# The return of expert outputs moved into the next pair's gate projection, its buffers shared, one more weight unit

## The chip, the cores and the metric

The kernel runs on one core of one Trainium2 chip. The metric is the device time of one execution in microseconds; the time before is the median of three runs. The engines are TensorE (PE in the profile, its weight loads PEld), VectorE (DVE), ScalarE (ACT), GpSimd (POOL) and SyncE (SP), which issues the weight transfers.

## The reference

A two-layer decoder trunk on 256 tokens of width 1024, in float32. Layer 1 of the reference (layer 0 in the code) is multi-scale retention with 4 heads, layer 2 (layer 1 in the code) is block attention with 8 heads over 256 tokens. Each is followed by a mixture of experts, which is what the change touches:

```python
g_val, g_idx = lax.top_k(g_prob, 1)
e_val, e_idx = lax.top_k(e_logits, EXPERT_TOPK)      # 2 of the 4 experts of one of 4 groups
hg = silu(einsum('td,edf->tef', t, w_gate[g])) * einsum('td,edf->tef', t, w_up[g])
y = y + einsum('tef,efd->td', hg * combine[:, g, :, None], w_down[g])
```

There are 16 experts of hidden width 512, and every token goes to two of them. A final RMS norm ends the trunk. The weights are about 250 MB, and the kernel reads them all.

## The kernel before, in words

**Order.** Retention, experts of layer 0, attention, experts of layer 1. The dense stages split each weight into two float32r parts (L337 to L341) and multiply three times (L345 to L347).

**Weights.** All weights pass through a ring of 1 MB units (class Ring, L158 and L147 are its issues). A unit is a [128, 2048] float32 tile, 8 KB in each partition. In an expert stage the ring has 19 slots of its own, further ones that other tiles leave (flex_slot, slot_v, h) and N_EXTRA more. SP issues the units in order; an issue waits until the last reader of its slot is done, and until the transfer eight issues earlier has landed.

**Expert pairs.** moe(layer) works through 8 pairs of experts. A pair has 12 units: gate, up and down, 4 each. Each expert takes up to 64 tokens, so the two experts of a pair fill the 128 rows of a tile, expert s in rows 64 s to 64 s + 63. The two sides are multiplied as 64-column matmuls (tile 128x64) side by side: expand (L982) for gate and up into a PSUM bank each (tag ps, 2 banks), project (L1010) for down into two banks (tag pt, 2 banks). Each float32 matmul is two instructions in the trace.

**Steps of one pair j** (loop at L1227), in TensorE's order, which is written out by hand here as is ScalarE's (manual_schedule); VectorE's, GpSimd's and SP's order is the framework's:

1. silu of the gate by ScalarE in two halves (L1204), then up (L982, 8 k steps), then gate() multiplies in two halves on VectorE (L1210).
2. turn_in: the tokens of pair j + 1, which were fetched into xn, are transposed by 4 + 4 transposes (L953) into two pt banks and written to xg, one half by VectorE (L940), the other by ScalarE in four pieces (L944).
3. turned: the hidden tile is transposed by 4 transposes into one ps bank (L997) and copied to hd, columns 0 to 255 by VectorE (L999) and 256 to 511 by ScalarE (L1000).
4. scatter: the return of pair j - 1, 8 matmuls of full width (L1029, L1030) which add its outputs to the four accumulators total, through the 0/1 matrix ST.
5. slots(j + 2): two small matmuls (L960) give the token numbers of pair j + 2, and pull (L947) lets GpSimd fetch these tokens from DRAM by an indirect DMA into xn.
6. project (L1010): the down projection.
7. parts: the outputs are split into yh by ScalarE (L1021) and yl by VectorE (L1022), four tiles of 2 KB each.
8. Gate of pair j + 1 (L982). In the last but one pair a branch for experts with more than 64 tokens (more, L1106) stands in the middle of it.

The return of the last pair follows its own down projection (L1259, or L1038 to L1071 in finish with the final norm).

**Waits.** The framework makes a wait for each dependence that it sees between instructions of different engines. For a tile of PSUM the rows below show which instructions of other engines a reader waited for.

**Buffers.** flex 2 and 3 hold the two float32r parts of the dense stages' input (8 KB each); in the expert stages flex 3 holds xn and xg together (held), and flex 0 to 2 are ring slots. Tiles of tag work (2 buffers of 2 KB) take the hidden tile and its transpose in turn.

Of the kernel before, what the change touches and what calls it, by code (L numbers as in the profile page):

```python
# [10 lines left out]
F32 = mybir.dt.float32  # L11
# [184 lines left out]
def trunk(ctx, tc, x, x_t, dense_in, moe_in, gain_in, par_in, fin_in, rot_in, dec_in, con_in, out):  # L196
    nc = tc.nc
    V = nc.vector
    N_BASE, N_FLEX, N_EXTRA = 20, 2, 0
# [13 lines left out]

    def x_parts():
        return flex(2, [128, KD, T], F32R, "xh"), flex(3, [128, KD, T], F32R, "xl")
# [51 lines left out]
    ident_b = const.tile([128, 128], BF16, name="ident_b")  # L267
# [192 lines left out]
    def retention():  # L460
        with tc.tile_pool(name="ret_w", bufs=2, reuse_waits="tile") as wpool:
# [98 lines left out]
            for n, (a, b, unit, pieces) in enumerate(FIRST):  # L560
# [3 lines left out]
                if n == 0:  # L564
# [14 lines left out]
            nc.gpsimd.affine_select(out=ident_b, in_=ones_b, compare_op=OP.is_equal, fill=0.0, base=0,  # L579
                                    pattern=[[-1, 128]], channel_multiplier=1)  # L580
# [187 lines left out]
    def router(layer, junk):  # L768
# [34 lines left out]
    def moe(layer):  # L803
        g0 = G_FFN[layer]
        with tc.tile_pool(name="extra", bufs=1, side="right", reuse_waits="tile") as late, \
# [172 lines left out]
            def expand(sides, xg, p, name, ks, weight, done):  # L978
                w = 128 // len(sides)
                for k in ks:  # L980
                    for s in sides:
                        nc.tensor.matmul(p[s * w:(s + 1) * w], xg[:, k, s * w:(s + 1) * w], weight(name, k, s),  # L982
                                         start=(k == 0), stop=(k == KD - 1))
                    done(name, k)
# [18 lines left out]
            def project(sides, hd, weight, done):  # L1003
                w = 128 // len(sides)
                yp = [pt(), pt()]
                for ks in ((0, 1), (2, 3)) if len(sides) > 1 else ((0,), (1,), (2,), (3,)):
                    for n in range(2):
                        for k in ks:
                            for s in sides:
                                nc.tensor.matmul(yp[n][s * w:(s + 1) * w], hd[:, k, s * w:(s + 1) * w],  # L1010
                                                 weight("d", k, s)[:, n * 512:(n + 1) * 512],
                                                 start=(k == 0), stop=(k == 3))
                    for k in ks:
# [65 lines left out]
            def slots(j, bank=pt):  # L1079
                RS[j], idx = slot_values(sel_of(j), [cs[:, tt, j] for tt in range(NT)],  # L1080
                                         [con[:, C_SELC + 12 * n:C_SELC + 12 * n + 12] for n in range(2)], bank)
                if j:
                    pull(idx, xn)
# [14 lines left out]
            def grow(j, name, ks):  # L1098
# [244 lines left out]
```

## Time and profile before

| | us |
|---|---|
| median of 3 runs | 742.85 (742.61 to 743.23) |
| the profiled execution | 742.91 |
| its span, first to last instruction | 740.9 |
| TensorE busy | 720.5 (97%) |
| VectorE busy | 320.1 (43%) |
| ScalarE busy | 270.4 (36%) |
| GpSimd busy | 35.9 (5%) |
| granted TensorE clock, mean | 0.997 of full |

The span is cut in 40 slices of 18.5 us in the page's second part; a digit is the busy share of a slice in tenths. The expert stages run from about 209 to 412 us (layer 0) and from about 527 us to the end (layer 1). In the timeline a line is one instruction or several alike behind each other: start, length until the last has ended, engine, line of the kernel, what is written from what, the shape, the count, and in brackets the idle time before and what ended it. Matmuls overlap, so the start of the next line, not the length, tells how long a group held TensorE.

### The profile page before, as it was taken

The page shows a single profiled execution, that of the slowest core. Times are in us where ns is not written, and L with a number is a line of the kernel's source. Part 1 is how long each engine was busy: PE and PEld are TensorE (multiplying, and loading weights), DVE is VectorE, ACT ScalarE, POOL GpSimd, SP SyncE. Part 2 cuts the span into 40 slices and gives each one's busy share as a digit, 9 for nine tenths or more (in the row PEclk, how much of TensorE's full clock was granted, in tenths as well). Part 3 has the DMA queues.
Part 4 walks back from the last instruction along what each step waited for, and adds up shares of the span by engine and source line. Part 5 has one row for each costly group of instructions (what it writes and reads, how often), then busy time and mean ns, then how long its engine had stood idle before and what let it go on. Part 6 is the DMA issues. An engine that isn't in the chain of part 4 may idle for free.

```text
span 740.9 us, 10093 instructions
## 1 busy us (share of the span) xinstructions
PE 720.5 (97%) x3652; PEld 430.1 (58%) x3652; DVE 320.1 (43%) x893; ACT 270.4 (36%) x550; POOL 35.9 (5%) x48
## 2 busy tenths in 40 slices
PE   8999999999999999999999999999999999999984
PEld 6988898887863434443343688888733344434431
DVE  4976688667661202211110677765721121112103
ACT  5667554667431111111110778674411111111112
POOL 0000000001000000000000003130010000000000
PEclk9999999999999999999999999999999999999998
DMA  8999646577879999999999799757899999999993
GB/s 246 421 420 420 228 145 243 207 278 274 323 283 388 422 419 419 419 423 419 419 421 404 315 422 421 290 211 303 318 397 421 420 421 418 423 419 421 420 410 122
DMA packets 43366, 263.24 MB, mean 355 GB/s; under 512 B 5695, under 2 KB 6975, under 8 KB 13616
## 3 DMA queue, kind: packets, MB, share of 16 engines
q1 hardware_dynamic: 40752, 256.85, 86.5%
q0 software_dynamic: 2560, 5.71, 2.1%
q8 instruction: 30, 0.49, 0.3%
q14 instruction: 24, 0.20, 0.1%
HBM read 263.12 MB, written 3.15 MB: 359 GB/s over the span
## 4 chain that ended last, share of the span: by engine, by line
PE 62%; DMA 34%; DVE 2%; issue 1%; SPq 0%; ACT 0%; DVEq 0%; POOLq 0%; ACTq 0%
DMA slot<-in_moe_dram 22%; PE ps L982 10%; PE acc L347 10%; PE acc L345 10%; PE acc L346 10%; DMA h<-in_moe_dram 8%; PE pt L1010 7%; DMA held<-rows,idx 2%; PE acc L383 2%; PE acc L381 2%; PE acc L382 2%; PE ps L794 1%; DMA slot<-in_dense_dram 1%; PE pt L953 1%; PE pt L884 1%; PE acc L1030 1%
## 5 line engine op out<-in xcount | busy, mean ns | idle before, releaser
L982 PE MATMUL ps<-slot,held 128*64 128x512 f32 x816 | 184.8, 594 | 2.0 <-DMA slot<-in_moe_dram 1.6
L982 PEld LDWEIGHTS ps<-slot,held 128*64 128x64 f32 x816 | 58.5, 137 | 116.7 <-issue 104.7
L341 DVE SCALAR_TENSOR_TENSOR wlo<-slot,gain,whi 128x512 fp32r<-128x512 f32 x144 | 107.0, 752 | 37.4 <-ACT whi L340 35.8
L340 ACT ACTIVATE whi<-slot,gain 128x512 fp32r<-128x512 f32 x144 | 102.9, 721 | 55.4 <-PE acc L346 37.0
L1210 DVE SCALAR_TENSOR_TENSOR gl<-ps,rs,gl 128x256 f32<-128x256 f32 x32 | 14.0, 480 | 194.5 <-PE ps L982 194.5
L1010 PE MATMUL pt<-slot,hd 128*64 128x512 f32 x416 | 96.2, 596 | 1.0 <-DVE idx L962 0.5
L345 PE MATMUL acc<-whi,xh 128*128 128x512 f32 x224 | 91.1, 407 | 0.6 <-ACT whi L340 0.6
L346 PE MATMUL acc<-whi,xl 128*128 128x512 f32 x224 | 87.6, 391 | 0.0
L347 PE MATMUL acc<-wlo,xh 128*128 128x512 f32 x224 | 87.5, 393 | 0.1
L1022 DVE TENSOR_TENSOR yl<-pt,yh 128x512 fp32r<-128x512 f32 x32 | 22.1, 691 | 99.9 <-ACT yh L1021 99.9
L1021 ACT ACTIVATE yh<-pt 128x512 fp32r<-128x512 f32 x32 | 19.1, 597 | 115.5 <-PE pt L1010 115.5
L1010 PEld LDWEIGHTS pt<-slot,hd 128*64 128x64 f32 x416 | 28.5, 137 | 53.1 <-issue 51.1
L944 ACT ACTIVATE held<-pt,gain 128x128 f32<-128x128 f32 x60 | 17.2, 368 | 102.5 <-PE pt L953 99.0
L1204 ACT ACTIVATE gl<-ps,rs 128x256 f32<-128x256 f32 x32 | 13.4, 470 | 106.3 <-PE ps L982 106.3
L347 PEld LDWEIGHTS acc<-wlo,xh 128*128 128x128 f32 x224 | 42.0, 188 | 10.0 <-DVE wlo L341 0.5
L345 PEld LDWEIGHTS acc<-whi,xh 128*128 128x128 f32 x224 | 42.2, 188 | 8.9 <-ACT whi L340 0.9
L346 PEld LDWEIGHTS acc<-whi,xl 128*128 128x128 f32 x224 | 42.2, 188 | 8.2
L338 DVE TENSOR_TENSOR wlo<-slot,whi 128x512 fp32r<-128x512 f32 x44 | 30.2, 689 | 21.0 <-ACT whi L337 18.2
L337 ACT ACTIVATE whi<-slot 128x512 fp32r<-128x512 f32 x44 | 27.8, 632 | 28.3 <-DVE wlo L338 16.3
L381 PE MATMUL acc<-xh,whi 128*128 128x256 f32 x128 | 35.9, 281 | 1.7 <-ACT whi L340 1.7
L383 PE MATMUL acc<-xh,wlo 128*128 128x256 f32 x128 | 36.2, 284 | 0.4 <-DVE wlo L341 0.3
L382 PE MATMUL acc<-xl,whi 128*128 128x256 f32 x128 | 35.6, 279 | 0.0
(226 smaller groups left out, 933.1 us busy)
## 6 DMA issues: line engine op xcount, KB each, us to landing
slot<-in_moe_dram SPq DMA_DIRECT2D x152, 1024.0 KB, 19.8
slot<-in_dense_dram SPq DMA_DIRECT2D x43, 1024.0 KB, 17.5
flex_slot<-in_moe_dram SPq DMA_DIRECT2D x22, 1024.0 KB, 19.8
slot_v<-in_moe_dram SPq DMA_DIRECT2D x8, 1024.0 KB, 19.6
h<-in_moe_dram SPq DMA_DIRECT2D x6, 1024.0 KB, 19.8
slot<-in_dense_dram SPq DMA_DIRECT2D x16, 256.0 KB, 6.4
rows<-h POOLq DMA_DIRECT2D x2, 1024.0 KB, 8.8
flex_slot<-in_moe_dram SPq DMA_DIRECT2D x4, 512.0 KB, 17.7
```

The costliest lines, as they stand in the source:

```text
L337: nc.scalar.activation(hi, w, AF.Copy)
L338: V.tensor_tensor(lo, w, hi.bitcast(F32), op=OP.subtract)
L340: nc.scalar.activation(hi, w, AF.Copy, scale=g)
L341: V.scalar_tensor_tensor(lo, w, g, hi.bitcast(F32), op0=OP.mult, op1=OP.subtract)
L345: nc.tensor.matmul(p, a, wh, start=start, stop=False)
L346: nc.tensor.matmul(p, l, wh, start=False, stop=False)
L347: nc.tensor.matmul(p, a, wl, start=False, stop=stop)
L381: nc.tensor.matmul(d, wh[:, s], xh[:, k], start=(k == 0 and c % 2 == 0), stop=False)
L382: nc.tensor.matmul(d, wh[:, s], xl[:, k], start=False, stop=False)
L383: nc.tensor.matmul(d, wl[:, s], xh[:, k], start=False, stop=(k == KD - 1 and c % 2 == 1))
L982: nc.tensor.matmul(p[s * w:(s + 1) * w], xg[:, k, s * w:(s + 1) * w], weight(name, k, s), start=(k == 0), stop=(k == KD - 1))
L1010: nc.tensor.matmul(yp[n][s * w:(s + 1) * w], hd[:, k, s * w:(s + 1) * w], weight("d", k, s)[:, n * 512:(n + 1) * 512], start=(k == 0), sto ...
```

## The change

- The return of pair j stands after the first two k steps of the gate of pair j + 1, and no longer before the down projection of pair j + 1.
- The fetch of pair j + 2 is issued after that return and no longer right after its slots.
- Up's last two k steps are done for columns 0 to 255 and then for columns 256 to 511.
- turn_in and turned alternate: four input transposes, two of the hidden tile, four, two. ScalarE copies the first half of the hidden tile, VectorE the second. In the last pair the second two hidden transposes stand inside the down projection (between).
- flex 3 is cut in two tiles of 4 KB, flex 3 (xg) and flex 4. Flex 4 holds in turn the fetched tokens (xn) and the first half of the split outputs (ylow); the second half uses the work tiles. The four ys tiles, one of two ST tiles and the constant ident_b go. Halves makes the two tiles look like one in the dense stages.
- N_EXTRA is 1: one more ring slot of 8 KB in the expert stages.

```diff
-    N_BASE, N_FLEX, N_EXTRA = 20, 2, 0
+    N_BASE, N_FLEX, N_EXTRA = 20, 2, 1
...
+    def rows_in():
+        return flex(4, [128, D], F32, "xn")
...
-        held = flex(3, [128, 2, D], F32, "held")
-        xn = held[:, 0]
-        xg = held[:, 1].rearrange("p (k j) -> p k j", k=KD)
+        xg = flex(3, [128, D], F32, "xg").rearrange("p (k j) -> p k j", k=KD)
+        xn = rows_in()
...
-            def turned(hh, hd, bank=ps):
+            def turned(hh, hd, t, n):
                 hv = hh.rearrange("t (k p) -> t k p", k=4)
-                t = bank()
-                for k in range(4):
-                    nc.tensor.transpose(t[:, k * 128:(k + 1) * 128], hv[:, k], ident)
                 tv = t.rearrange("p (k j) -> p k j", k=4)
-                V.tensor_copy(hd[:, 0:2], tv[:, 0:2])
-                nc.scalar.activation(hd[:, 2:4], tv[:, 2:4], AF.Copy)
-                return hd
+                for k in (2 * n, 2 * n + 1):
+                    nc.tensor.transpose(tv[:, k], hv[:, k], ident)
+                s = slice(2 * n, 2 * n + 2)
+                if n:
+                    V.tensor_copy(hd[:, s], tv[:, s])
+                else:
+                    nc.scalar.activation(hd[:, s], tv[:, s], AF.Copy)
...
+                low = flex(4, [128, 2, 512], F32R, "ylow")
                 for n in range(2):
-                    ys.append([t1(name, [128, 512], F32R, bufs=4, tag="ys") for name in ("yh", "yl")])
+                    ys.append([work(name, F32R) if n else low[:, i] for i, name in enumerate(("yh", "yl"))])
...
-                    grow(j, "u", range(0, 8))
+                    grow(j, "u", range(0, 6))
+                    for s in halves:
+                        grow(j, "u", range(6, 8), s)
                     gate(hh, GU[j, "u"], rs)
+                    hd, t, idx, between = work("hd").rearrange("p (k j) -> p k j", k=4), ps(), None, None
                     if j + 1 < NP:
                         for n in range(2):
                             turn_in(xn, xg, range(4 * n, 4 * n + 4), COLS[n])
-                    hd = turned(hh, work("hd").rearrange("p (k j) -> p k j", k=4))
-                    if ahead:
-                        scatter(*ahead)
-                    if j + 2 < NP:
-                        slots(j + 2, ps)
-                    yp = project(both, hd, weight_of(j), done_of(j))
-                    st = transposed_select(rs, t1("ST", [128, T], F32R, bufs=2))
-                    if j + 2 < NP:
-                        ahead = parts(yp), st
-                        grow(j + 1, "g", range(0, 8))
-                    elif j + 1 < NP:
-                        ahead = parts(yp), st
-                        grow(j + 1, "g", range(0, 4))
+                            turned(hh, hd, t, n)
+                        if j + 2 < NP:
+                            idx = slots(j + 2, ps)
+                    else:
+                        turned(hh, hd, t, 0)
+
+                        def between():
+                            turned(hh, hd, t, 1)
+
+                    st = transposed_select(rs, t1("ST", [128, T], F32R))
+                    yp = project(both, hd, weight_of(j), done_of(j), between)
+                    if j + 1 < NP:
+                        ys = parts(yp)
+                        grow(j + 1, "g", range(0, 2))
+                        scatter(ys, st)
+                        if j + 2 < NP:
+                            xn = rows_in()
+                            pull(idx, xn)
+                            grow(j + 1, "g", range(2, 8))
+                            continue
+                        grow(j + 1, "g", range(2, 4))
```

project calls between() once, after the first half of its first output bank.

## Rows read from the trace of the kernel before

**Rows 1.** The page: TensorE's busy line, the transfers' share in 40 slices, the chain that ended last by engine.
```profile
PE 720.5 (97%) x3652; PEld 430.1 (58%) x3652; DVE 320.1 (43%) x893; ACT 270.4 (36%) x550; POOL 35.9 (5%) x48
...
DMA  8999646577879999999999799757899999999993
...
PE 62%; DMA 34%; DVE 2%; issue 1%; SPq 0%; ACT 0%; DVEq 0%; POOLq 0%; ACTq 0%
```
**Rows 2.** TensorE's timeline over one pair in the middle of layer 1: the end of up, input transposes (L953), hidden transposes (L997), the first two and (by the next line's start) all matmuls of the return, slots (L960), down projection (L1010), gate of the next pair.
```profile
566.55 5.32 PE L982 MATMUL ps<-slot,held 128*64 128x512 f32 x24
571.80 1.09 PE L953 MATMUL pt<-ident,held 128*128 128x128 f32 x8
572.73 0.64 PE L997 MATMUL ps<-ident,gl 128*128 128x128 f32 x4
573.12 0.48 PE L1029 MATMUL acc<-yh,ST 128*128 128x512 f32 x1
573.44 0.39 PE L1030 MATMUL acc<-yl,ST 128*128 128x512 f32 x1
...
575.05 0.21 PE L960 MATMUL ps<-cs,S 128*128 128x13 bf16 x2
575.19 1.08 PE L1010 MATMUL pt<-slot,hd 128*64 128x512 f32 x4
...
582.11 5.32 PE L982 MATMUL ps<-slot,held 128*64 128x512 f32 x24
```
**Rows 3.** The chain of waits in order of time: the gate and up matmuls of the next pair as one piece (start, length, what).
```profile
582.28 13.73 PE ps L982 x64
```
**Rows 4.** TensorE's timeline at the end of layer 0 and of layer 1: the start of the last pair's gate, the branch, the last up matmuls, the last turn (layer 1), the end of the moved return (layer 1), the start of the last down projection; then, in layer 1, the end of that projection and the return behind it.
```profile
385.01 1.89 PE L982 MATMUL ps<-slot,held 128*64 128x512 f32 x8
...
388.77 5.37 PE L982 MATMUL ps<-slot,held 128*64 128x512 f32 x24 [0.16 <-PEq L1106]
...
398.41 1.94 PE L982 MATMUL ps<-slot,held 128*64 128x512 f32 x8 [0.54 <-DMA slot<-in_moe_dram]
...
403.59 3.65 PE L1010 MATMUL pt<-slot,hd 128*64 128x512 f32 x16
...
702.81 1.89 PE L982 MATMUL ps<-flex_slot,held 128*64 128x512 f32 x8
...
716.87 1.94 PE L982 MATMUL ps<-slot,held 128*64 128x512 f32 x8 [0.54 <-DMA slot<-in_moe_dram]
...
719.54 0.74 PE L997 MATMUL ps<-ident,gl 128*128 128x128 f32 x4 [0.73 <-DVE gl L1210]
...
721.74 0.40 PE L1030 MATMUL acc<-yl,ST 128*128 128x512 f32 x1
722.07 1.08 PE L1010 MATMUL pt<-slot,hd 128*64 128x512 f32 x4
...
728.13 1.03 PE L1010 MATMUL pt<-slot,hd 128*64 128x512 f32 x4
729.09 0.50 PE L1029 MATMUL acc<-yh,ST 128*128 128x512 f32 x1
729.42 0.39 PE L1030 MATMUL acc<-yl,ST 128*128 128x512 f32 x1
```
**Rows 5.** Busy time in one stretch of 4 us at the start of the experts of layer 0: us, PE, PEld, DVE, ACT, POOL busy (instructions), granted clock, DMA share, GB/s.
```profile
212.00:216.00 4.00, 4.00 (x36) 3.29 (x36) 3.55 (x21) 1.02 (x4) 0.00 (x0) 1.00 0.50 199
```
**Rows 6.** The page's groups of instructions: the split of the down projection's output, on VectorE and on ScalarE (busy us, mean ns of one, idle before).
```profile
L1022 DVE TENSOR_TENSOR yl<-pt,yh 128x512 fp32r<-128x512 f32 x32 | 22.1, 691 | 99.9 <-ACT yh L1021 99.9
L1021 ACT ACTIVATE yh<-pt 128x512 fp32r<-128x512 f32 x32 | 19.1, 597 | 115.5 <-PE pt L1010 115.5
```
**Rows 7.** VectorE and ScalarE in the timeline of the same pair as rows 2: the gate's two halves, the first input copy, the two halves of the hidden tile's copy.
```profile
572.00 0.88 DVE L1210 SCALAR_TENSOR_TENSOR gl<-ps,rs,gl 128x256 f32<-128x256 f32 x2 [12.49 <-PE ps L982]
...
572.79 0.68 DVE L940 TENSOR_TENSOR held<-pt,gain 128x512 f32<-128x512 f32 x1
...
573.40 0.42 DVE L999 COPY hd<-ps 128x256 f32<-128x256 f32 x1
...
574.01 0.40 ACT L1000 ACTIVATE hd<-ps 128x256 f32<-128x256 f32 x1
```
**Rows 8.** The view of waits (who waited for whom: us in total, times, longest) for readers of a PSUM bank that another instruction uses at other columns. L708 reads columns 0 to 127 and L709 columns 128 to 255 of an attention score tile, whose columns 128 to 383 L705 writes.
```profile
ACT hd L1000 <- DVE hd L999: 17.3, 2, 9.1
...
ACT slot L709 <- DVE slot L708: 3.1, 3, 1.0
...
DVE slot L708 <- PE ps L705: 1.6, 3, 0.7
...
DVE held L940 <- ACT held L944: 0.4, 2, 0.2
```
**Rows 9.** Float32 matmuls of 256 columns in the attention stage: two of them and the start of what follows on TensorE.
```profile
483.33 0.59 PE L736 MATMUL ps<-slot,slot 128*128 128x256 f32 x2
...
483.76 0.38 PE L737 MATMUL ps<-slot,slot 128*128 128x128 f32 x2
```
**Rows 10.** The token fetches (L947), all 14: us from the start of the fetch on GpSimd to its landing.
```profile
DMA to landing us min/median/max: 8.1/8.6/9.1
```
**Rows 11.** TensorE's timeline in the first pair of layer 0: input transposes after the fetch, and the down projection.
```profile
231.22 1.06 PE L953 MATMUL pt<-ident,held 128*128 128x128 f32 x8 [0.65 <-DMA held<-rows,idx]
...
233.23 7.09 PE L1010 MATMUL pt<-slot,hd 128*64 128x512 f32 x32 [0.48 <-DVE idx L962]
```

More of the change, by code (lines that the diff above doesn't have):

```diff
@@ L212, in flex_slot, with __init__, __getitem__ @@
         return flex(n, [128, 2048], F32, f"flex_slot{n}")
+    class Halves:
+        def __init__(self, parts):
+            self.parts = parts
+        def __getitem__(self, at):
+            p, ks, *rest = at
+            if isinstance(ks, int):
+                return self.parts[ks // 4][(p, ks % 4, *rest)]
+            n = ks.start // 4
+            assert ks.stop <= 4 * n + 4
+            return self.parts[n][(p, slice(ks.start - 4 * n, ks.stop - 4 * n), *rest)]
     def x_parts():
-        return flex(2, [128, KD, T], F32R, "xh"), flex(3, [128, KD, T], F32R, "xl")
+        return flex(2, [128, KD, T], F32R, "xh"), Halves([flex(3 + n, [128, 4, T], F32R, f"xl{n}") for n in range(2)])
+    def rows_in():
+        return flex(4, [128, D], F32, "xn")
     def acc():
@@ L976, in transposed_select, with expand @@
                 return st
-            def expand(sides, xg, p, name, ks, weight, done):
+            def expand(sides, xg, p, name, ks, weight, done, at=slice(0, FE)):
                 w = 128 // len(sides)
@@ L981, in expand @@
                     for s in sides:
-                        nc.tensor.matmul(p[s * w:(s + 1) * w], xg[:, k, s * w:(s + 1) * w], weight(name, k, s),
-                                         start=(k == 0), stop=(k == KD - 1))
-                    done(name, k)
+                        nc.tensor.matmul(p[s * w:(s + 1) * w, at], xg[:, k, s * w:(s + 1) * w],
+                                         weight(name, k, s)[:, at], start=(k == 0), stop=(k == KD - 1 and at.stop == FE))
+                    if at.stop == FE:
+                        done(name, k)
             def glu(gp, up, rs, hh):
@@ L991, in glu, with project @@
                 return hh
-            def turned(hh, hd, bank=ps):
+            def turned(hh, hd, t, n):
                 hv = hh.rearrange("t (k p) -> t k p", k=4)
-                t = bank()
-                for k in range(4):
-                    nc.tensor.transpose(t[:, k * 128:(k + 1) * 128], hv[:, k], ident)
                 tv = t.rearrange("p (k j) -> p k j", k=4)
-                V.tensor_copy(hd[:, 0:2], tv[:, 0:2])
-                nc.scalar.activation(hd[:, 2:4], tv[:, 2:4], AF.Copy)
-                return hd
-            def project(sides, hd, weight, done):
+                for k in (2 * n, 2 * n + 1):
[5 more added lines that the diff above has]
+                    nc.scalar.activation(hd[:, s], tv[:, s], AF.Copy)
+            def project(sides, hd, weight, done, between=None):
                 w = 128 // len(sides)
@@ L1012, in project @@
                                                  start=(k == 0), stop=(k == 3))
+                        if between:
+                            between()
+                            between = None
                     for k in ks:
@@ L1081, in slots @@
                                          [con[:, C_SELC + 12 * n:C_SELC + 12 * n + 12] for n in range(2)], bank)
-                if j:
-                    pull(idx, xn)
+                return idx
             def weight_of(j):
@@ L1096, in done_of, with grow @@
                 return done
-            def grow(j, name, ks):
+            def grow(j, name, ks, at=slice(0, FE)):
                 if (j, name) not in GU:
                     GU[j, name] = ps()
-                expand(both, xg, GU[j, name], name, ks, weight_of(j), done_of(j))
+                expand(both, xg, GU[j, name], name, ks, weight_of(j), done_of(j), at)
             def more():
@@ L1190, in more @@
                         half = [e2_[:, n * FE:(n + 1) * FE] for n in range(4)]
-                        lhd = turned(glu(*lp2, lrs, half[0]), e0[:, D:D + 512].rearrange("p (k j) -> p k j", k=4), pt)
+                        lhd = e0[:, D:D + 512].rearrange("p (k j) -> p k j", k=4)
+                        lhh, lt = glu(*lp2, lrs, half[0]), pt()
+                        for n in range(2):
+                            turned(lhh, lhd, lt, n)
                         y = half[2:]
@@ L1207, in gate @@
             def gate(hh, up, rs):
-                for c in range(2):
-                    s = slice(c * 256, (c + 1) * 256)
+                for s in halves:
                     V.scalar_tensor_tensor(hh[:, s], up[:, s], rs[:, 1:2], hh[:, s], op0=OP.mult, op1=OP.mult)
+            halves = [slice(c * 256, (c + 1) * 256) for c in range(2)]
             with tc.manual_schedule(engines={mybir.EngineType.PE}):
@@ L1233, in moe @@
                         nc.scalar.activation(small.tile([128, 1], F32, name="root1"), ident[:, 0:1], AF.Sqrt)
-                    grow(j, "u", range(0, 8))
+                    grow(j, "u", range(0, 6))
+                    for s in halves:
+                        grow(j, "u", range(6, 8), s)
                     gate(hh, GU[j, "u"], rs)
+                    hd, t, idx, between = work("hd").rearrange("p (k j) -> p k j", k=4), ps(), None, None
                     if j + 1 < NP:
```

6 lines of the change are left out of this document (1 added, 5 removed).

## The prediction

> **What bounds the kernel now.** I read the page first. TensorE is busy 97% of the span and the transfers are nearly full in both expert layers, so either could be the limit, and the chain of waits gives 34% to DMA [rows 1]. The reader is to see next that this share misleads. TensorE's timeline of one expert pair in the middle of layer 1 has no hole: up matmuls from 566.55, transposes at 571.80, the return (scatter) at 573.12, the down projection at 575.19, the next gate projection at 582.11 [rows 2]. The chain has 64 gate and up matmuls in 13.73 us, 0.2145 each [rows 3]. So up ends at E = 566.55 + 24 x 0.2145 = 571.70, the down projection starts at P = 575.19, 3.49 after E, of which the return takes 573.12 to 575.05 = 1.93 and the rest 1.56.
>
> Does TensorE wait for weights at all? Only in the last pair of each layer [rows 4]. Layer 0's last gate starts at 385.01; 64 matmuls and the 0.33 hole of the branch (388.77 against 385.01 + 16 x 0.2145 = 388.44) would end up at 399.07; it ends at 398.41 + 8 x 0.2145 = 400.13. Layer 1: 702.81 gives 716.87, and it is 718.59. So the transfers hold TensorE 1.06 and 1.72 us, 2.8 in all; everything else in the expert stages is TensorE's own order.
>
> **The extra weight unit.** Transfers do stand idle for a moment at the start of each expert stage (share 0.50 in layer 0, [rows 5]); a unit more in flight there can bring later units forward. It can shorten only those 2.8 us. I value it at nothing, since the moved return alone puts the last up matmuls behind the last landings (below); its bounds are 0 and 2.8.
>
> **The return inside the gate projection.** Eight matmuls at (575.05 - 573.44)/7 = 0.23 stay eight matmuls. What changes is the neighbours. Today it stands behind transposes of the same 128-column shape and pays 0.09. Now it stands between 64-column matmuls. The end of layer 1 shows both edges [rows 4]: down projection to return, last group 728.13 + 4 x 0.2145 = 728.99, return at 729.09, second matmul 0.33 later where 0.23 is usual, so 0.20; return to down projection, 721.74 + 0.23 = 721.97 against 722.07, and about 0.05 lost in the first group, so 0.15. In its new place the return costs 8 x 0.23 + 0.35 = 2.19, 0.26 more, seven times a layer. Bounds 0 and 0.5. Its operands are no wait: the last one is ready 0.28 + 0.60 + 0.69 = 1.6 us after the down projection (ScalarE's split, then VectorE's, [rows 6]; 0.28 is worked out below) and is used at 1.72 + 0.2 + 0.9 = 2.8.
>
> **The turns.** Now: four input transposes, two of the hidden tile, four, two, the next slots, the down projection. Three waits decide. (a) Hidden transposes need the first gated half. Up's last quarter is split so that this half could be gated early, but both halves lie in one PSUM bank. The rows say that the program waits by bank: a VectorE read of columns 0 to 127 waited for the matmul on columns 128 to 383 (L708 for L705), a ScalarE read of other columns waited for that VectorE read (L709 for L708), and so did the two halves of the hidden tile's copy (L1000 for L999) and of the input's (L940 for L944) [rows 8]. So the gate starts as now, at 572.00, 0.30 after E [rows 7], and the first hidden transpose at 0.95 after E, as in the last pair (718.59 to 719.54, [rows 4]); today eight input transposes hide that, in the new order four (until 0.63) do not. (b) The first two hidden transposes end at 1.15 (0.10 each, (573.12 - 572.73)/4, [rows 2]); ScalarE starts 0.28 later, as VectorE does at 573.40, and copies for 0.40 [rows 7]: 1.83. The other two write the same bank, so by the same rule they wait for that copy: 1.88 to 2.08. No row shows a TensorE write held by a reader of other columns; without this wait they follow the input transposes at 1.55. (c) Slots 0.14, down projection at E + 2.22. That is 0.66 more than 1.56 (bounds 0, and 0.8). The input's first copy, 572.79 plus 0.68, is done by then.
>
> The PSUM rule matters here. The Trainium skill, page "PSUM — Partial Sum Buffer", section "PSUM bank collisions raise a hardware error", says that two engines may not touch one bank in the same quadrant of partitions at once, whatever the columns, and that accesses are to be guarded by bank. By it the wait in (b) is needed too and the sum is the one below; by columns alone it would be that of the third rival.
>
> **Edits at nothing.** The half-width matmuls: 256 columns in f32 run at (483.76 - 483.33)/2 = 0.215 each, their weight loads hidden [rows 9], so sixteen at half width replace eight at the same time. The upper bound is a bare load in each of eight steps, at most the 0.14 of a two-matmul slots step, 1.1 us a pair. The Trainium skill, page "TensorE: Matmul & The Clock Gate", section "The mechanism", says that weight loads overlap running matmuls only in another row group; both sides here share theirs. By it the loads would be bare; the 0.2145 of [rows 3] speaks against it. The fetch of the next tokens is now queued on POOL behind the return's first half: 1.72 + 0.2 + 0.9 + 0.3 = 3.1 after the down projection; with at most 9.1 to landing [rows 10] it is there at 12.2, and is wanted after gate, return and up at 13.73 + 2.19 + 0.1 = 16.0. That cover is 3.8. Nothing else of weight is queued on POOL. SP's issues keep their order, the extra one among them. Splitting the buffers and dropping one constant touch no chain.
>
> **First and last pair.** The first pair has no gate wait (up ended while the tokens were fetched) but a hole of about half a microsecond before its down projection. By (b): 231.22 + 0.53 + 0.20 + 0.28 + 0.40 + 0.05 + 0.20 + 0.14 = 233.02 against 233.23 [rows 11]: 0.2 gained. In the last pair the down projection starts at 0.95 + 0.20 + 0.28 + 0.40 + 0.05 = 1.88 after E, and the two later transposes stand inside it at 0.35 (two shape changes as above, two at 0.10).
>
> **Sum.** End of the last up matmuls without weight waits, then the changes: -0.2, six turns at 0.66 = 3.96, seven returns at 2.19 less six at 1.93 = 3.75; together +7.51. Layer 0: 399.07 + 7.51 + 1.88 + 0.35 = 408.81 against the down projection's start at 403.59 [rows 4]: +5.2. Layer 1: 716.87 + 9.74 = 726.61 against 722.07: +4.5. The last up matmuls would begin near 404.9 and 722.7, well behind their weights' landings at 398.41 and 716.87, and the down units behind them are wanted later than now, so no weight wait is left. Layer 0's loss passes on whole, since the attention stage starts from its result. 742.91 + 9.7 = 752.7 for an execution like the profiled one, which is 0.06 above the median: 752.6.
>
> **Rivals.**
> - *Only the gate waits by bank* (TensorE isn't held by ScalarE's copy). For: no row shows that wait. Against: every pair of engines in [rows 8] does wait. The down projection starts at E + 1.89, 0.33 less in twelve pairs and 0.2 in two: 748.2.
> - *Loads become bare in the half-width matmuls.* 1.1 x 16 = 18 more: about 770. Against it: [rows 3, 9].
> - *Columns are told apart.* The gate's first half runs beside up's second, turned and input transposes hide each other's copies, as the order is meant: twelve turns 0.61 less, two last pairs 0.85 less, the first pairs 0.3 less: 743.0, no change.
> - *The other side: the return fills the time in which TensorE waited for weights.* As the last rival, and the edges of the return inside the gate cost nothing: 14 x 0.26 less, 739.4, faster. It decides from the point where a moved return plus its edges cost less than the 2.8 us of waits. For: those waits and the bare 0.95 after the last up are in the rows. Against: the edges in [rows 4] and the waits in [rows 8].
> - *The change doesn't do what it says* (no room for the unit, or a late fetch) is inside these, as the unit is worth nothing in the first.
>
> **Chances and range.** Forecast 0.64, gate alone 0.10, bare loads 0.04, columns told apart 0.11, faster 0.11. About 0.2%, 1.5 us, is what a measurement of this kernel tells from no change. Faster takes the fifth and a sliver of the fourth, 0.12; the rest of the fourth and a little beside it is no change, 0.12; slower 0.76. The forecast's own range, with 0.1 either way on twelve turns and on fourteen returns, is 749.8 to 755.4. The range that leaves out no more than the faster case, the bare loads and a rest is 742.8 to 756.
>
> **What would show it.** In the changed profile: down projection about 2.2 after the last up matmul of a middle pair, with the second pair of hidden transposes waiting for ScalarE's copy and the first for the gate; the gate starting after both halves; returns of about 2.2 from gate to gate; no weight waits in the last pairs; the fetch landed before it is wanted. I am wrong if the gate starts while up still runs, if a middle pair takes 24.2 us or less, or if TensorE still waits for weights at the end.

## The result and the profile after

The changed kernel takes 752.76 us (median of 4 runs, 752.58 to 753.29) where the kernel before took 742.73 in the same comparison: ratio 1.0137, 95% interval 1.012 to 1.0155. It is slower by 10.0 us. The profiled execution has 752.77 us, a span of 750.7 (740.9 before) and a granted clock of 0.996 (0.997).

The page of the changed kernel, the lines that answer to [rows 1]:

```profile
PE 729.5 (97%) x3780; PEld 439.7 (59%) x3780; DVE 321.5 (43%) x893; ACT 272.0 (36%) x550; POOL 35.4 (5%) x47
...
DMA  7999546478799999999998997567999999999981
...
PE 3%; DVE 1%; ACT 0%; DVEq 0%; issue 0%
```

TensorE is still busy 97%, of a span that grew with it, so this share can't show where 10 us went. Nor can the chain of waits: its shares add up to 4% of the span, where the kernel before has 99% [rows 1]. It was followed back only to 719.16, the last pair's gate behind the branch, and says nothing of the time ahead of that. That DMA is missing in it is therefore no finding; what became of the waits for weights is read from TensorE's timeline below.

The timeline of one pair in the middle of layer 1, with TensorE, VectorE, ScalarE and GpSimd; it answers to [rows 2, 7]. L964 is an input transpose, L1009 a hidden one, L971 the slots, L1023 the down projection, L993 gate and up, L1046 and L1047 the return, L1228 the gate's multiplication, L1014 ScalarE's copy:

```profile
578.48 0.66 PE L964 MATMUL pt<-ident,xn 128*128 128x128 f32 x4
578.67 0.88 DVE L1228 SCALAR_TENSOR_TENSOR gl<-ps,rs,gl 128x256 f32<-128x256 f32 x2 [11.71 <-PE ps L993]
579.30 0.41 PE L1009 MATMUL ps<-ident,gl 128*128 128x128 f32 x2 [0.17 <-DVE gl L1228]
...
579.55 0.60 PE L964 MATMUL pt<-ident,xn 128*128 128x128 f32 x4
579.75 0.38 ACT L1014 ACTIVATE hd<-ps 128x256 f32<-128x256 f32 x1 [7.20 <-PE ps L1009]
...
580.19 0.44 PE L1009 MATMUL ps<-ident,gl 128*128 128x128 f32 x2
580.46 0.20 PE L971 MATMUL ps<-cs,S 128*128 128x13 bf16 x2
580.59 1.08 PE L1023 MATMUL pt<-slot,hd 128*64 128x512 f32 x4
...
587.51 1.89 PE L993 MATMUL ps<-slot,xg 128*64 128x512 f32 x8
589.32 0.50 PE L1046 MATMUL acc<-ylow,ST 128*128 128x512 f32 x1
...
591.03 0.99 POOL L958 DMA_INDIRECT xn<-rows,idx  x1 [24.09 <-PE acc L1047]
...
591.37 5.37 PE L993 MATMUL ps<-slot,xg 128*64 128x512 f32 x24
...
603.55 0.66 PE L964 MATMUL pt<-ident,xn 128*128 128x128 f32 x4
```

Read it from one input transpose to the next: 603.55 - 578.48 = 25.07 a pair. The kernel before has 595.94 - 571.80 = 24.14, from this row of its next pair and the one in [rows 2]:

```profile
595.94 1.09 PE L953 MATMUL pt<-ident,held 128*128 128x128 f32 x8
```

From the first input transposes to the down projection it is 2.11; before it was 575.19 - 571.80 = 3.39, of which the return took 1.93, so 1.46 [rows 2]. The gate starts 0.19 after the input transposes, as before, although up is split. The second pair of hidden transposes starts at 580.19, just behind ScalarE's copy (579.75 + 0.38 = 580.13). The return costs from 587.51 + 8 x 0.2145 = 589.23 to 591.37, 2.14.

The end of layer 1 on TensorE's timeline, answering to [rows 4]:

```profile
717.06 1.94 PE L993 MATMUL ps<-slot,xg 128*64 128x512 f32 x8
719.16 1.94 PE L993 MATMUL ps<-slot,xg 128*64 128x512 f32 x8 [0.16 <-PEq L1122]
...
727.77 1.93 PE L993 MATMUL ps<-slot,xg 128*64 128x256 f32 x16
730.43 0.41 PE L1009 MATMUL ps<-ident,gl 128*128 128x128 f32 x2 [0.74 <-DVE gl L1228]
731.31 1.94 PE L1023 MATMUL pt<-slot,hd 128*64 128x512 f32 x8 [0.47 <-ACT hd L1014]
733.18 0.44 PE L1009 MATMUL ps<-ident,gl 128*128 128x128 f32 x2
733.55 5.37 PE L1023 MATMUL pt<-slot,hd 128*64 128x512 f32 x24
738.85 0.50 PE L1046 MATMUL acc<-ylow,ST 128*128 128x512 f32 x1
```

No up matmul waits for a transfer any more. In the last pair nothing hides the waits of the turn: 0.74 for the gate and 0.47 for the copy.

Most experiments move single microseconds, and executions of one kernel differ by as much outside the expert stages. So each is also read by its own profiled stages: from the first gate matmul of a layer to its last down projection, from there to layer 1's first gate matmul, and to the end of the span. The last column is the turn of a middle pair of layer 1, from the first input transposes to the down projection, without the return. All are differences of starts in TensorE's timelines; the column to the end is good to 0.1 only, as the spans are given to 0.1.

| kernel | layer 0 | layer 1 | between | to the end | turn |
|---|---|---|---|---|---|
| before | 188.65 | 189.36 | 129.12 | 18.8 | 1.46 |
| changed | 193.13 | 193.47 | 129.65 | 19.4 | 2.11 |
| return alone | 193.87 | 193.78 | 129.12 | 18.9 | 2.08 |
| turns alone | 190.15 | 190.21 | 129.94 | 19.4 | 2.05 |
| up whole | 193.05 | 193.41 | 129.92 | 19.3 | 2.11 |
| two banks | 191.34 | 191.34 | 129.64 | 19.3 | 1.86 |
| four banks | 188.51 | 188.88 | 129.65 | 19.4 | 1.57 |
| no extra slot (1st, 2nd) | 193.11, 193.11 | 193.47, 193.47 | 129.66, 129.66 | 20.1, 20.1 | |
| last return (1st, 2nd) | 187.81, 187.82 | 187.78, 188.52 | 129.41, 129.43 | 18.8, 18.8 | |
| last return, first and last pair split | 187.33 | 187.25 | 129.42 | 19.1 | |
| last return, last pair split | 186.94 | 186.96 | 129.45 | 18.9 | |

The changed kernel's excess is 4.48 + 4.11 + 0.53 + about 0.5 and 0.12 ahead of the first gate: about 9.8, the difference of the spans.

### The profile page after: what moved, and what is told of

It is laid out like the page before. It is cut to its first block, busy times and chain, and to the rows that moved or that the text cites. A ratio compares the mean times of both kernels' runs of the same rounds, so it can differ in the third digit from the quotient of the medians.

```text
span 750.7 us, 10355 instructions
## 1 busy us (share of the span) xinstructions
PE 729.5 (97%) x3780; PEld 439.7 (59%) x3780; DVE 321.5 (43%) x893; ACT 272.0 (36%) x550; POOL 35.4 (5%) x47
## 5 line engine op out<-in xcount | busy, mean ns | idle before, releaser
L993 PE MATMUL ps<-slot,xg 128*64 128x512 f32 (+1 forms) x904 | 181.2, 542 | 0.3 <-PEq L1122 0.3
L993 PEld LDWEIGHTS ps<-slot,xg 128*64 128x64 f32 x904 | 65.2, 137 | 105.5 <-issue 91.9
L1023 PE MATMUL pt<-slot,hd 128*64 128x512 f32 x416 | 93.6, 596 | 0.5 <-ACT hd L1014 0.5
L1228 DVE SCALAR_TENSOR_TENSOR gl<-ps,rs,gl 128x256 f32<-128x256 f32 x32 | 14.0, 479 | 183.2 <-PE ps L993 183.2
L1023 PEld LDWEIGHTS pt<-slot,hd 128*64 128x64 f32 x416 | 28.5, 137 | 52.3 <-issue 50.8
L1014 ACT ACTIVATE hd<-ps 128x256 f32<-128x256 f32 x16 | 6.1, 383 | 112.2 <-PE ps L1009 112.2
L1039 DVE TENSOR_TENSOR ylow<-pt,ylow 128x512 fp32r<-128x512 f32 x16 | 11.1, 692 | 75.0 <-ACT ylow L1038 75.0
L352 DVE TENSOR_TENSOR wlo<-slot,whi 128x512 fp32r<-128x512 f32 x48 | 32.9, 690 | 23.5 <-ACT whi L351 20.7
L351 ACT ACTIVATE whi<-slot 128x512 fp32r<-128x512 f32 x48 | 30.3, 631 | 31.3 <-DVE wlo L352 15.9
L1038 ACT ACTIVATE ylow<-pt 128x512 fp32r<-128x512 f32 x16 | 9.6, 597 | 77.4 <-PE pt L1023 77.4
## 6 DMA issues: line engine op xcount, KB each, us to landing
slot_v<-in_moe_dram SPq DMA_DIRECT2D x8, 1024.0 KB, 19.1
```

The costliest lines, as they stand in the source:

```text
L351: nc.scalar.activation(hi, w, AF.Copy)
L352: V.tensor_tensor(lo, w, hi.bitcast(F32), op=OP.subtract)
L993: nc.tensor.matmul(p[s * w:(s + 1) * w, at], xg[:, k, s * w:(s + 1) * w], weight(name, k, s)[:, at], start=(k == 0), stop=(k == KD - 1 and ...
```

## The experiments

**The return alone.** The kernel before, with nothing but the return moved.

```diff
-                    if ahead:
-                        scatter(*ahead)
...
+                        ys = parts(yp)
+                        grow(j + 1, "g", range(0, 2))
+                        scatter(ys, st)
+                        grow(j + 1, "g", range(2, 8))
```

> The kernel before with the return alone moved into the gate projection of the next pair, behind the first two k steps; turns, buffers, slots and the issue of the fetch as before. Theory: the return was the cover of the hidden tile's copies; without it the down projection waits for them and comes about 2.2 us after the last up matmul, as in the changed kernel, so the moved return alone costs as much as the whole change: about 752.6, ratio 1.013. Rival: the parts add up, the return costs only its two edges, 0.26 us in 14 pairs less the 2.8 us of waits for weights that it fills: about 744.2, ratio 1.002.

752.41 us, ratio 1.0141 (1.0124 to 1.0157). The timeline of a middle pair, its turn and the start of the next:

```profile
579.20 1.09 PE L953 MATMUL pt<-ident,held 128*128 128x128 f32 x8
...
580.13 0.64 PE L997 MATMUL ps<-ident,gl 128*128 128x128 f32 x4
580.19 0.68 DVE L940 TENSOR_TENSOR held<-pt,gain 128x512 f32<-128x512 f32 x1
...
580.80 0.42 DVE L999 COPY hd<-ps 128x256 f32<-128x256 f32 x1
...
581.28 1.08 PE L1010 MATMUL pt<-slot,hd 128*64 128x512 f32 x4 [0.48 <-DVE hd L999]
...
588.20 1.89 PE L982 MATMUL ps<-slot,held 128*64 128x512 f32 x8
...
592.06 3.65 PE L982 MATMUL ps<-slot,held 128*64 128x512 f32 x16
...
604.23 1.09 PE L953 MATMUL pt<-ident,held 128*128 128x128 f32 x8
```

The down projection waits for VectorE's copy of the hidden tile (L999), which stands behind its copy of the input (L940). Before, the return filled just this time, and no wait was to be seen. One edit costs as much as the whole change: the return was a cover, that is, work that kept TensorE busy while it would have waited for the copies.

**The turns alone.** The kernel before with the new order of transposes and copies and up in halves, the return in its old place.

```diff
-                    grow(j, "u", range(0, 8))
+                    grow(j, "u", range(0, 6))
+                    for s in halves:
+                        grow(j, "u", range(6, 8), s)
...
                             turn_in(xn, xg, range(4 * n, 4 * n + 4), COLS[n])
-                    hd = turned(hh, work("hd").rearrange("p (k j) -> p k j", k=4))
+                            turned(hh, hd, t, n)
```

> The kernel before with the changed turns alone: input and hidden transposes alternate, up's last two k steps in halves, ScalarE copies the first half of the hidden tile. The return stays where it was, behind the turns. Theory: the first hidden transposes wait for the gate and the second pair for ScalarE's copy, but the return then covers VectorE's copy, so only the waits on TensorE before the return show: about 0.4 us a pair, 2.8 us in layer 0 and 2.1 in layer 1, about 747.6, ratio 1.0065. Rival: the turns are what costs, wherever the return stands: 750 or more, ratio 1.010. Rival, the turns are free: 743, ratio 1.000.

746.46 us, ratio 1.0066 (1.0048 to 1.0083). The ratio is the expected one, but partly by luck: the stages are 1.50 and 0.85 longer where 2.8 and 2.1 were expected, and the rest of the excess lies outside them, 0.8 between the layers, some 0.5 behind the last down projection and 0.3 ahead of the first gate. (The two transposes that this order puts inside the last down projection fall behind the stages, in each layer.) In the stages two terms are not as expected:

```profile
573.76 0.66 PE L953 MATMUL pt<-ident,held 128*128 128x128 f32 x4
...
575.03 0.38 ACT L1003 ACTIVATE hd<-ps 128x256 f32<-128x256 f32 x1 [7.20 <-PE ps L998]
...
575.47 0.44 PE L998 MATMUL ps<-ident,gl 128*128 128x128 f32 x2
...
575.67 0.49 PE L1034 MATMUL acc<-yh,ST 128*128 128x512 f32 x1
...
577.75 1.08 PE L1012 MATMUL pt<-slot,hd 128*64 128x512 f32 x4
```

The return starts 1.91 after the first input transposes (573.12 - 571.80 = 1.32 before): 0.59 a pair, not 0.4, as the waits now stand ahead of the return. Given back are the waits for weights and 0.62 in the first pair of layer 0. So, in a middle pair, the new turns alone cost 0.59 a pair, the return alone 0.62 and both together 0.65: the two don't add, because each takes the cover from the same chain from gate to down projection. The moved return pays its edges besides.

**Up in whole width.**

```diff
-                    grow(j, "u", range(0, 6))
-                    for s in halves:
-                        grow(j, "u", range(6, 8), s)
+                    grow(j, "u", range(0, 8))
```

> The changed kernel with up's last two k steps in whole width, not in halves. Theory: the halves are useless because the gate waits for the whole bank; they cost nothing or about 0.07 us a pair (16 pairs): 751.7 to 752.8, the down projection still 2.2 us after the last up matmul. Rival, columns told apart: the halves let the gate start 0.43 us earlier; without them the down projection comes 0.3 to 0.4 later in every pair, 5 us slower, about 758.

752.85 us, ratio 1.0149 (1.0129 to 1.0168), and the turn is 2.11 again. The stages are 0.08 and 0.06 shorter, some 0.01 a pair. In one bank the halves bring nothing and cost next to nothing.

**The hidden transposes in two banks.**

```diff
+                t = t() if callable(t) else t
...
-                    hd, t, idx, between = work("hd").rearrange("p (k j) -> p k j", k=4), ps(), None, None
+                    hd, t, idx, between = work("hd").rearrange("p (k j) -> p k j", k=4), ps, None, None
```

> The changed kernel with the two pairs of hidden transposes in a bank each. Theory: in the changed kernel the second pair is held by ScalarE's copy of the first pair's half, in the same bank. With a bank of its own it runs straight behind the second input transposes (about 1.65 us after the last up matmul instead of 1.88), and the slots that follow take the bank of the first pair and wait for ScalarE's copy there, so the down projection comes about 2.0 after the last up matmul instead of 2.21: 0.2 in 12 pairs, 2.4 us faster than the changed kernel, about 750.4, ratio 1.010. Rival: the bank isn't what holds the second pair (TensorE is behind with its own work, or VectorE's input copy holds it): no change, 752.8.

748.16 us, ratio 1.0091 (1.0073 to 1.0109). The same part of the timeline:

```profile
575.80 0.66 PE L964 MATMUL pt<-ident,xn 128*128 128x128 f32 x4
...
577.08 0.38 ACT L1015 ACTIVATE hd<-ps 128x256 f32<-128x256 f32 x1 [7.20 <-PE ps L1010]
...
577.31 0.38 PE L1010 MATMUL ps<-ident,gl 128*128 128x128 f32 x2
...
577.66 1.08 PE L1024 MATMUL pt<-slot,hd 128*64 128x512 f32 x4
```

The second pair runs at 577.31 while ScalarE copies until 577.46: the wait is gone with the shared bank. It was worth 0.25 a pair in 14 pairs, and 0.36 in one pair of layer 1 (below): 3.9 in the stages, where 2.4 was expected (0.2 in 12 pairs).

**Up's halves in two banks as well.**

```diff
-                                         weight(name, k, s)[:, at], start=(k == 0), stop=(k == KD - 1 and at.stop == FE))
+                                         weight(name, k, s)[:, at], start=(k == 0), stop=(k == KD - 1 and (name == 'u' or at.stop == FE)))
...
+                if name == "u":
+                    if (j, name) not in GU:
+                        GU[j, name] = ps(), pt()
+                    for n in range(2):
+                        if at.start <= n * 256 < at.stop:
+                            expand(both, xg, GU[j, name][n], name, ks, weight_of(j), done_of(j), halves[n])
+                    return
```

> As the kernel with two banks for the hidden transposes, and up's two halves of columns in a bank each (every up matmul is then 256 columns wide). Theory: the first half of the gate no longer waits for up's second half; it starts while up still runs, the first hidden transposes no longer wait after the first four input transposes, and the down projection comes about 1.7 us after the last up matmul in a middle pair and some 0.9 earlier in the last pairs: about 745 to 746, ratio 1.003 to 1.004, so most of the loss goes and the rest is the return's edges. Against it, if half-width matmuls cost 0.07 us for each eight, six more such groups a pair: 7 us back, about 752. Rival: the bank isn't what the gate waits for: no gain at all, 752 or more.

742.53 us, ratio 1.0015 (1.0003 to 1.0027), below the 745 to 746 that were expected; 2.2 of the difference had already come with the two banks (748.16 for 750.4).

```profile
571.22 1.03 PE L993 MATMUL pt<-slot,xg 128*64 128x256 f32 x8
571.52 0.48 DVE L1236 SCALAR_TENSOR_TENSOR gl<-ps,rs,gl 128x256 f32<-128x256 f32 x1 [10.88 <-PE ps L993]
572.19 0.66 PE L964 MATMUL pt<-ident,xn 128*128 128x128 f32 x4
...
572.68 0.38 PE L1010 MATMUL ps<-ident,gl 128*128 128x128 f32 x2
...
573.76 1.08 PE L1024 MATMUL pt<-slot,hd 128*64 128x512 f32 x4
```

The gate's first half starts at 571.52, while up's second half runs until 572.1; no row of the kernel before or of the changed one shows that. The turn falls to 1.57. Without the two waits the stages are 4.6 us shorter each than in the changed kernel, about as much as the change had added (4.5 and 4.1). What remains of the change there, the edges of the returns on one side and on the other the waits for weights that are gone and shorter first and last pairs, about cancels.

This edit does one thing more than part the banks: it also closes the accumulation of each half by itself (stop), where the changed kernel closes the bank once, with the second half. No run parts the two for up. In [rows 8] both score matmuls close themselves, and the reader of the one still waited for the other in the same bank, so the bank is the likelier reason. For the hidden transposes the edit was the bank alone.

**Without the extra slot**, twice, and beside it the changed kernel once more.

```diff
-    N_BASE, N_FLEX, N_EXTRA = 20, 2, 1
+    N_BASE, N_FLEX, N_EXTRA = 20, 2, 0
```

> The changed kernel without the extra weight slot (N_EXTRA 0). Theory: the slot is worth nothing, because the later return already puts the last up matmuls of each layer 5 us behind their weights' landings: no change from the changed kernel, 752.8 give or take 0.5, a ratio to the kernel before of 1.013. Rival: the slot is what removed the waits for weights in the last pairs (1.06 and 1.72 us in the kernel before): they come back in whole or in part, up to 755.5, ratio up to 1.017, and TensorE's timeline shows a wait for a transfer before the last up matmuls again.

754.37 us, ratio 1.016 (1.0139 to 1.0182). The theory's number failed, the stages were as it said, so both kernels ran on one chip:

> The changed kernel without the extra weight slot, once more, because its first median lay 1.6 us above the changed kernel's, taken against other runs. Theory: the slot is worth nothing and the 1.6 us come from run to run outside the expert stages: the two medians agree within 0.5, and from the first gate matmul to the last down projection it takes 193.1 and 193.5 us again. Rival: the slot is worth 1.6 us: the median lies 1.6 above the changed kernel's again.

> The changed kernel once more, beside the one without the extra slot, on one chip. Theory: 752.8 give or take 1.5, ratio 1.0135 to 1.016; from the first gate matmul of a layer to its last down projection 193.13 us in layer 0 and 193.47 in layer 1, as in its first profile.

752.67 us for the changed kernel, ratio 1.0144 (1.0116 to 1.0173), and 754.18 without the slot, 1.0163 (1.0138 to 1.0188): 1.5 between the medians again, as the rival said, though the two intervals overlap. It isn't the weights: the stages agree to 0.02. In these two profiles the first gate stands at 215.94 and 215.97, and the 0.8 between the spans (751.5 and 752.3) lies behind the last instruction. The time from issue to landing of the output's transfers (L1088), first of the changed kernel, then without the slot:

```profile
DMA to landing us min/median/max: 2.1/2.4/2.7
```

```profile
DMA to landing us min/median/max: 2.1/2.8/3.5
```

Both are issued last at 747.6. Without the slot the output is sent from another ring slot and lands 0.8 later. What makes it land later, and where the other 0.7 between the medians is, stays open.

**Only the last return moved.** The return goes into the gate where TensorE waited for weights; the first pair turns its hidden tile earlier, and ScalarE copies first.

```diff
+                        turn_in(xn, xg, range(0, 4), COLS[0])
+                        if not j:
+                            turned(hh, hd)
+                        turn_in(xn, xg, range(4, 8), COLS[1])
+                    if j:
+                        turned(hh, hd)
...
-                        ahead = parts(yp), st
-                        grow(j + 1, "g", range(0, 4))
+                        ys, ahead = parts(yp), None
+                        grow(j + 1, "g", range(0, 2))
+                        scatter(ys, st)
+                        grow(j + 1, "g", range(2, 4))
```

> The kernel before with three small edits: only the return of the last but one pair of each layer moves into the gate projection of the last pair, where TensorE waits for weights; the first pair, which has no return, transposes the hidden tile between its two groups of input transposes; ScalarE copies the first half of the hidden tile and VectorE the second. Theory: the moved return fills the waits for weights (1.06 us in layer 0, 1.72 in layer 1) at the price of the hidden copies' cover in that pair (0.9): layer 0 gains 0.2 and layer 1 0.9, the first pairs 0.35 each: about 741.1, ratio 0.9977. Rival: the cover costs more than the waits give, and the first pairs are held by the fetch: 743 or more.

> The version with the moved last return alone once more, beside the one above on one chip. Theory: stages of 187.8 us in both layers again, a median 1.5 to 2 below the kernel before's, ratio 0.9975, and 1.9 above the version that also splits the last pair. Rival: 0.999 again, no difference that the runs can tell.

741.18 us, ratio 0.999 (0.9981 to 1.0), and 741.42, ratio 0.9996 (0.9985 to 1.0007). The stages are 0.84 and 1.58 shorter in the first profile, more than expected (0.55 and 1.25); in the second layer 1 is 0.7 longer than in the first, and the medians show less still. Those 0.7 are the first pair's: its token fetch took 9.5 us to land, 1.2 more than in the first profile, and TensorE waited 1.15 for it.

**That, with banks of their own** for up's halves and the hidden transposes, first in the first and last pair, then in the last alone. Both hidden pairs stand ahead of the projection. The second version:

```diff
+                    GU[j, name] = (ps(), pt()) if name == "u" and j == NP - 1 else ps()
...
+                    if j + 1 == NP:
+                        for turn in turned(hh, hd, ps, True):
+                            turn()
```

> The kernel before with the last return moved into the last gate (as in the third small version), and with up's halves of columns and the two pairs of hidden transposes in banks of their own in the first and the last pair of each layer, where nothing covers the gate's and the copies' waits. Theory: in the last pair the down projection comes about 1.2 us after the last up matmul instead of 2.15, in the first pair some 0.4 earlier (TensorE is then held by the fetch): 1.4 a layer, 2.8 in all, against the version with the moved return alone: about 738.4, ratio 0.9955. Rival: the splits don't help because the waits end elsewhere (ScalarE's copy of the first half, the fetch): 741, ratio 0.999.

740.25 us, ratio 0.9986 (0.9971 to 1.0002). The stages are 0.48 and 0.53 shorter than with the moved return alone, where 1.4 was expected. In the first pair of layer 0 the down projection came later, not earlier: TensorE waited 1.34 for the fetch. The fetch took 9.8 us to land in this profile and 8.7 in the one with the moved return alone, so what the split is worth in a first pair isn't shown. It was left out there:

> As the version with banks of their own in the first and the last pair, but in the last pair alone; the first pair as in the version with the moved return alone, since in the first pair TensorE waited 1.34 us for the fetch and the split gained nothing there. Theory: from the first gate matmul to the last down projection 186.9 us in layer 0 and 186.9 in layer 1 (187.81 and 187.78 less 0.93 for the last pair), 1.75 and 2.45 less than in the kernel before; a median 3.5 to 4 below the kernel before's, ratio 0.995. Rival: what the profiled stages gain doesn't reach the median, as with the last version: ratio 0.998 to 1.000.

740.4 us, ratio 0.9987 (0.9972 to 1.0001). The end of its layer 0:

```profile
401.29 1.06 PE L982 MATMUL pt<-slot,held 128*64 128x256 f32 x8
402.28 0.44 PE L1009 MATMUL ps<-ident,gl 128*128 128x128 f32 x2
403.00 0.44 PE L1009 MATMUL ps<-ident,gl 128*128 128x128 f32 x2 [0.28 <-DVE gl L1229]
403.36 3.65 PE L1023 MATMUL pt<-slot,hd 128*64 128x512 f32 x16
```

The down projection starts 1.21 after up (401.29 + 0.86 = 402.15), and both stages are as expected to 0.06: 1.7 and 2.4 shorter than before. The median is only 1.5 lower, and the ratio's interval includes 1: it isn't shown to be faster. In this profile the first gate stands at 216.42, against 214.94 before and 213.63 in the version with both pairs split, though nothing ahead of it was edited. That spread hides a gain of this size; its cause was not looked for.

## Why the prediction was right, point by point

The forecast was 752.6 and the time is 752.76. By its own steps:

- **The return inside the gate**, 2.19 forecast: 2.14, and the 24 matmuls behind it take 5.37 where 5.32 is usual, so 2.19. The return alone shows it free of the other edits: 588.20 + 8 x 0.2145 = 589.92 to 592.06 is 2.14 too, and its pair takes 604.23 - 579.20 = 25.03.
- **Turn (a), the gate waits by bank**: right. It starts 0.19 after the input transposes with up split and 0.20 with up whole, and early only where each half has its own bank (and its own close).
- **Turn (b), the second hidden pair waits for ScalarE's copy**: right, and shown by the two banks. This was the step without a row. The Trainium skill, page "PSUM — Partial Sum Buffer", section "PSUM bank collisions raise a hardware error", asks for a guard by bank; the 0.25 a pair that a second bank gives back is what that guard cost here. Whether the chip itself would have stood the overlap, no run here shows.
- **Turn (c), the down projection 0.66 later**: 2.11 - 1.46 = 0.65. A pair: 0.92 forecast, 0.93 measured. In the last pair of layer 1 it comes 731.31 - (727.77 + 16 x 0.107) = 1.8 after up, 1.88 forecast.
- **Half-width matmuls at nothing**: right, 0.01 a pair.
- **The extra unit at nothing**: right for the weights, whose waits are gone with and without it. That the output's transfer would land earlier with the slot, and the medians differ by 1.5, was not foreseen.
- **The first pair, -0.2**: mis-sized. It is 232.73 - 215.06 = 17.67 against 233.23 - 214.94 = 18.29 in layer 0, and 17.67 against 18.34 in layer 1: 0.62 and 0.67 gained. The step counted from the input transposes and took the 0.65 of waiting for the fetch [rows 11] as fixed. But the landing of this fetch moved. It is issued 7.1 us after the first gate matmul in both kernels; in layer 0 it took 9.06 to land before (first row, from the chain of waits) and 8.6, until 230.7, in the changed kernel (the other rows); in layer 1 it took 9.0 and 7.9:

```profile
222.02 9.06 DMA held<-rows,idx
```

```profile
222.15 1.08 POOL L958 DMA_INDIRECT xn<-rows,idx  x1 [15.09 <-DVE rs L980]
...
230.85 0.63 PE L964 MATMUL pt<-ident,xn 128*128 128x128 f32 x4
...
232.73 7.09 PE L1023 MATMUL pt<-slot,hd 128*64 128x512 f32 x32
```

  With the transposes that early the first pair's turn is held as a middle pair's is: the down projection starts 2.41 after up's last matmul has started, in a middle pair 2.42. So the prediction's "no gate wait" doesn't hold here either. Over all profiles the first pair's fetch took from 6.1 to 9.8 us to land; what moves it was not tested, and how much of the 0.62 and 0.67 is the change's own stays open.
- **The transposes inside the last projection, 0.35**: mis-sized. From the down projection to the return it is 738.85 - 731.31 = 7.54 against 7.02: 0.52.
- **The last but one pair of layer 1**: missed. There the gate starts 0.55 after the input transposes, and the turn takes 0.36 longer. It does so with up whole and without the slot, and not with two banks. VectorE's wait for up's last matmul ends at 703.99, 0.41 before the multiplication starts; in the middle pair above it ends 0.06 before. So up isn't what held the gate there, and the trace shows no later event that let it go: the cause stays open.

```profile
703.85 0.66 PE L964 MATMUL pt<-ident,xn 128*128 128x128 f32 x4
704.40 0.88 DVE L1228 SCALAR_TENSOR_TENSOR gl<-ps,rs,gl 128x256 f32<-128x256 f32 x2 [12.14 <-PE ps L993]
```

- **The fetch's cover, 3.8**: issued at 591.03, landed after at most 8.6 and wanted at 603.55: 3.9.

The middle pairs, which make most of the sum, came out as worked out, by the mechanism that was named. The misses are -0.9 in the first pairs and +0.7 in the other two; that these nearly cancel, and the sum stands to 0.1 (9.7 forecast, 9.8 in the spans), is luck. A slip in the range: 0.1 on each of 26 terms is 2.6, so 750.0 to 755.2 and not 749.8 to 755.4; it decides nothing. The rivals that tell columns apart (743.0 and 739.4) fall with turn (a); their 743.0 is about what the four banks give (742.53), and the gate-only rival's 748.2 is what the two banks give (748.16), but that rival falls with turn (b). The bare loads fall with up whole.

## What to carry to other kernels

Before a piece of work is moved off a chain that goes from one engine to another and back, ask what it covers there: the return was worth 0.6 us a pair as a cover, and that, with 0.26 for its edges and not its own length, was the price of moving it. A tile that is split so that its reader can start early gained here only once the halves lay in different PSUM banks, since in this program's waits a bank is one thing. Two edits that each uncover the same chain cost hardly more together than one alone (0.65 against 0.59 and 0.62), so the parts of such a change must be tried one by one, and not added.

## What was not expected of the hardware

- The time ahead of the first expert stage varied between profiled executions from 213.63 to 216.42 us, in kernels that don't differ there, and from 214.11 to 215.30 in two profiles of the same one (the last return moved).
- The token fetch of the first pair, issued about 7 us after the first gate matmul, landed 6.1 to 9.8 us after its issue.
- The output's transfers of 256 KB each landed after up to 2.7 us from one buffer and up to 3.5 from another.
